# Softmax factors through DRAM, a reordered end of the last layer, and a second weight set asked for sooner, in a two-layer hybrid attention encoder

## The chip, the cores and the metric

The kernel runs on one NeuronCore of a Trainium2 chip, as one program. The metric is device microseconds (us) of one execution; lower is better. A core has five engines that run at once, each through its own instructions in order: TensorE (PE in the profile; its weight loads are PEld) multiplies matrices, VectorE (DVE) and ScalarE (ACT) work element by element and read TensorE's results out of PSUM, GpSimd (POOL) works on SBUF alone, and SyncE (SP) issues most transfers. ACT and POOL issue transfers too, and those of POOL can add to what they write. Instructions of different engines wait for each other by semaphores. PSUM has eight banks of 512 fp32 columns by 128 partitions.

## The reference, cut to what matters

For 512 tokens of 1024 channels, two layers do this (all fp32):

```
proj = x @ w_in                      # queries, keys, values of mixers A and B, two gates
oa = banded_attention(qa, ka, va)    # exp(s - m) @ v / denominator; 8 heads
ob = sum over 3 dilated groups g of weight_g * (exp(s_g - m_g) @ v_g / denominator_g)
h  = (sigmoid(gate_a) * (oa @ w_branch_a) + sigmoid(gate_b) * (ob @ w_branch_b)) @ w_out
x  = layer_norm(alpha * x + h) * ln1_g + ln1_b
ple = sigmoid(x @ w_ple_gate + b) * (p @ w_ple)
x  = layer_norm(alpha * x + relu(x @ w_up)**2 @ w_down + ple) * ln2_g + ln2_b
```

What the change touches: the factors of each token and head (1 / denominator for mixer A; for mixer B the group's softmax weight over its denominators) that multiply the attention sums, the last layer norm with the writing of the output, and the hand-over of `p @ w_ple` to the second layer.

## The kernel before, in words

**Products.** Every fp32 operand is cut into a high part that TensorE takes in its faster fp32 mode and a rest (`split`, L236); a product is three matmuls (high by high, rest by high, high by rest; `mm3` L287). Weights come from DRAM in sets of 128x1024, fetched by SP (`fetch` L252) into three buffers `wst`, and split by `prep` (L261) into three buffers `whi`, `wlo`, two sets ahead of their use (`LOOK`). The sets listed in `LATER` are split by ACT and an adding transfer that POOL issues (`split_later`, L240). Most of these sets belong to the attention block.

**Start.** Eight transfers bring x by 128 channels each into `xs` (four buffers), and each is split; the first weight set is asked for after the first of them (L349 to L355), the others as the first products need them. Only where the code says `manual_schedule` is the order of an engine that of the program; elsewhere Tile's scheduler puts each engine's instructions in the order in which its own simulation finds them ready.

**Attention block** (L358 to L889). Projections ("fill") and the steps of attention units are woven into one order for TensorE, written out by hand: a forecast `fc` (L173) keeps a guessed time and guessed busy stretches of the other engines, and a unit's next step is issued when its condition holds in that guess, delayed further by the table `LEAVE`. `unit_a` (L511, four per layer) and `unit_b` (L594, six per layer) do scores, softmax, transposes of the probabilities and the products with v. Their sums lie as heads by tokens (64 channels of two heads on the partitions, tokens in the columns), while the denominators lie as tokens by heads. `widened` (L493) has ACT copy a unit's 8 factors of each token out to 128x512, `token_scaled` (L498) has TensorE transpose them by four 128x128 transposes into a PSUM bank `R`, and DVE multiplies the sums `f` by it. `unit_a` does this once at its end and splits the product into `OA`; `mix_b` (L704, two per layer) does it for each of its three groups and adds the groups up into `OB`. The products with `OA` (`ya`, in the filler) come late in the block and those with `OB` (`yb`) after it.

**Between the layers.** At the end of layer 0, while the last rows are normed, `embedding` (L1096) computes `p @ w_ple` for layer 1 into `ple` tiles that stay in SBUF through the attention of layer 1; rows go to DRAM (`kept`); the first set of the next layer is split with POOL's adding transfer and its product is begun (`start_by_halves`, L322).

**Down products.** `Down` (L974) multiplies by seven products (a scheme of Strassen's kind) for each quarter q of the hidden channels. `product(q, n)` (L1051) runs two row blocks s of 12 matmuls of 512 columns each; `gather` (L1078) then adds each result to y. After the last quarter's product 3, layer 1 ends with products 4, 5 and 6 in this order (L1301 to L1350), both s of each. Rows are four blocks y[0] to y[3] of 128 tokens: product 4 completes y[0] and y[1], products 5 and 6 complete y[2] and y[3]. `Tokens` (L898) has the moments and statistics of the layer norm: DVE's moments by halves, its aggregate, a reciprocal, ACT's square root, one step of refinement; then centring, scaling, adding the last bias, and writing `out`.

## Time and profile before

| | us |
|---|---|
| median of 3 runs (1530.86 to 1531.6) | 1531.06 |
| the profiled execution's own time | 1530.95 |
| its span, first to last instruction | 1529.2 |
| TensorE busy | 1506.9 (99%) |
| VectorE busy | 1030.7 (67%) |
| ScalarE busy | 768.2 (50%) |
| GpSimd busy | 250.9 (16%) |

The profiled execution takes 1.75 us more than its span, for what lies around the first and last instruction. A matmul's row lasts from its start to its modelled end and overlaps the next one's, so what a matmul costs TensorE is read from start to start. A row with "x4" stands for four instructions in a run; its length goes from the first's start to the last's end.

### The profile page before, as it was taken

How to read it: one execution, taken by the hardware profiler on the slowest of the kernel's cores; microseconds unless marked ns; L12 is line 12 of the kernel's file. 1: busy time of each engine (PE TensorE's matmuls, PEld its weight loads, DVE VectorE, ACT ScalarE, POOL GpSimd, SP SyncE). 2: the span in 40 equal slices, each digit the busy share in tenths (PEclk: the TensorE clock that was granted, in tenths of full speed). 3: DMA queues.
4: the chain of work that ended last, by engine and by line, in shares of the span. 5: the costliest groups of instructions: out<-in, count | busy, mean ns of one | idle time of the engine just before them, and what ended most of it. 6: DMA issues, size and time to landing. Idle time of an engine off the chain costs nothing.

```text
span 1529.2 us, 19607 instructions
## 1 busy us (share of the span) xinstructions
PE 1506.9 (99%) x7374; PEld 1249.8 (82%) x7374; DVE 1030.7 (67%) x1761; ACT 768.2 (50%) x1254; POOL 250.9 (16%) x221
## 2 busy tenths in 40 slices
PE   9999999999999999999999999999999999999996
PEld 7888888888888888888888888888888888888885
DVE  5865564458568777686868655544585876767868
ACT  5887674344344443444558776643442444444342
POOL 1221220110011120202022112211100201111022
PEclk9999999999999999999999999999999999999998
DMA  7644655345612414151455456565455233231403
GB/s 243 144 109 117 147 138 191 99 138 152 206 56 86 135 53 155 42 159 62 105 169 138 113 123 150 126 188 156 150 151 181 69 110 111 85 123 56 150 0 97
DMA packets 54592, 190.52 MB, mean 125 GB/s; under 512 B 6625, under 2 KB 7009, under 8 KB 54497
## 3 DMA queue, kind: packets, MB, share of 16 engines
q1 hardware_dynamic: 43200, 151.74, 29.8%
q0 software_dynamic: 10576, 37.23, 13.0%
q8 instruction: 58, 0.95, 0.2%
q10 hardware_dynamic: 720, 0.30, 0.1%
q14 instruction: 38, 0.30, 0.1%
HBM read 155.16 MB, written 4.19 MB: 104 GB/s over the span
## 4 chain that ended last, share of the span: by engine, by line
PE 87%; DVE 6%; ACT 2%; DMA 2%; issue 2%; POOL 0%; SPq 0%; POOLq 0%; ACTq 0%; DVEq 0%
PE dn L1065 17%; PE ps_up L291 8%; PE ps_up L289 8%; PE ps_up L290 8%; PE wo L297 2%; PE pg L297 2%; PE pg L295 2%; PE pg L296 2%; PE wo L296 2%; PE wo L295 2%; PE pta L451 1%; PE sb L473 1%; PE sa L478 1%; PE ya L289 1%; PE ya L291 1%
## 5 line engine op out<-in xcount | busy, mean ns | idle before, releaser
L237 ACT CAST whi<-wst 128x1024 fp32r<-128x1024 f32 (+2 forms) x120 | 121.1, 1010 | 261.6 <-PE ps_up L290 115.4
L238 DVE TENSOR_TENSOR wlo<-wst,whi 128x1024 fp32r<-128x1024 f32 (+2 forms) x120 | 146.1, 1222 | 142.3 <-ACT whi L237 131.9
L289 PE MATMUL ps_up<-xhi,whi 128*128 128x512 f32 x512 | 199.2, 389 | 0.0
L290 PE MATMUL ps_up<-xlo,whi 128*128 128x512 f32 x512 | 199.2, 389 | 0.0
L291 PE MATMUL ps_up<-xhi,wlo 128*128 128x512 f32 x512 | 199.2, 389 | 0.0
L1038 POOL TENSOR_TENSOR hr<-r 128x512 f32<-128x512 f32 x64 | 102.2, 1597 | 550.2 <-ACT r L1030 529.7
L290 PEld LDWEIGHTS ps_up<-xlo,whi 128*128 128x128 f32 x512 | 96.1, 188 | 20.0
L291 PEld LDWEIGHTS ps_up<-xhi,wlo 128*128 128x128 f32 x512 | 96.1, 188 | 19.9
L289 PEld LDWEIGHTS ps_up<-xhi,whi 128*128 128x128 f32 x512 | 96.1, 188 | 19.9
L237 ACT CAST whi<-raw 128x1024 fp32r<-128x1024 f32 x56 | 58.0, 1052 | 97.0 <-PE ps_up L290 64.1
L237 ACT CAST dhi<-raw 128x1024 fp32r<-128x1024 f32 x56 | 58.7, 1052 | 82.2 <-PE dn L1065 59.5
L1084 DVE TENSOR_TENSOR y<-y,dn 128x512 f32<-128x512 f32 x96 | 65.2, 682 | 38.5 <-PE dn L1065 38.5
L244 POOL DMA_DIRECT2D wlo<-wst x54 | 47.8, 885 | 253.6 <-ACT wlo L243 150.9
L1018 DVE TENSOR_TENSOR raw<-raw,raw 128x1024 f32<-128x1024 f32 x64 | 86.4, 1350 | 0.2
L238 DVE TENSOR_TENSOR wlo<-raw,whi 128x1024 fp32r<-128x1024 f32 x56 | 68.2, 1220 | 14.1 <-ACT whi L237 14.1
L238 DVE TENSOR_TENSOR dlo<-raw,dhi 128x1024 fp32r<-128x1024 f32 x56 | 69.2, 1239 | 5.4 <-ACT dhi L237 5.4
L242 ACT CAST whi<-wst 128x1024 fp32r<-128x1024 f32 x54 | 56.5, 1046 | 30.3 <-PE ps_start L290 6.9
L243 ACT ACTIVATE wlo<-whi 128x1024 fp32r<-128x1024 f32 x54 | 57.3, 1061 | 0.8
L1065 PE MATMUL dn<-whi,smh 128*128 128x512 f32 x128 | 50.2, 394 | 0.7 <-DVE y L1084 0.7
L1065 PE MATMUL dn<-wlo,smh 128*128 128x512 f32 x128 | 50.5, 395 | 0.1
L1065 PE MATMUL dn<-whi,sml 128*128 128x512 f32 x128 | 49.9, 390 | 0.0
L1065 PE MATMUL dn<-dhi,smh 128*128 128x512 f32 x128 | 49.9, 390 | 0.0
(860 smaller groups left out, 4049.2 us busy)
## 6 DMA issues: line engine op xcount, KB each, us to landing
wst<-wst SPq DMA_DIRECT2D x187, 512.0 KB, 3.5
raw<-wst SPq DMA_DIRECT2D x64, 512.0 KB, 4.3
wlo<-wst POOLq DMA_DIRECT2D x54, 512.0 KB, 4.6
y<-rows POOLq DMA_DIRECT2D x14, 512.0 KB, 7.7
row<-rows SPq DMA_DIRECT2D x7, 512.0 KB, 8.4
wst<-wst SPq DMA_DIRECT2D x9, 256.0 KB, 2.7
xs<-xT SPq DMA_DIRECT2D x8, 256.0 KB, 6.2
y<-xN SPq DMA_DIRECT2D x4, 512.0 KB, 6.6
```

The lines of the kernel that those rows point to most:

```text
L237: nc.scalar.copy(hi, src)
L238: nc.vector.tensor_tensor(lo, src, hi.bitcast(F32), ALU.subtract)
L289: nc.tensor.matmul(ps, w[0][:, s], x[0], start=start, stop=False, skip_group_check=part)
L290: nc.tensor.matmul(ps, w[0][:, s], x[1], start=False, stop=False, skip_group_check=part)
L291: nc.tensor.matmul(ps, w[1][:, s], x[0], start=False, stop=stop, skip_group_check=part)
L295: nc.tensor.matmul(ps, x[0], w[0][:, c], start=start, stop=False)
L296: nc.tensor.matmul(ps, x[0], w[1][:, c], start=False, stop=False)
L297: nc.tensor.matmul(ps, x[1], w[0][:, c], start=False, stop=stop)
L1018: nc.vector.tensor_tensor(to, to, other, ALU.add)
L1038: nc.gpsimd.tensor_tensor(h.rearrange("p s t -> p (s t)"), r, r, ALU.mult)
L1065: nc.tensor.matmul(ps[s], a[:, k, tok], w[b][:, cols], start=first and not (k or m), stop=k == 3 and m == 2, skip_group_check=True)
L1084: return nc.vector.tensor_tensor(to, to, ps, ALU.subtract if n in (2, 4, 5) else ALU.add)
```

## The change

In the attention block a unit's factors are transposed as they are, 8 (mixer A) or 24 (mixer B) columns at once, by one transpose (`in_rows`); ACT copies the rows to SBUF and issues a transfer of them to DRAM; SP issues two transfers for each 128x512 tile `R`, which read a row of factors and repeat it over 64 partitions (`in_columns`). The multiplication by `R` and what follows it are put off by `LATENCY` = 7 us of the forecast (`scaled_a`, `mixed_b`); `f` has two buffers and `R` three. The first products with `OA` wait in the written order for the put-off steps. `LEAVE` is another table, of 34 entries where there were 26.

At the start `xs` has eight buffers, and the second weight set is asked for after the second piece of x.

At the end of layer 0 the `ple` tiles are written to DRAM (four of 256 KB) and read back in layer 1 after its attention.

The end of layer 1 goes by row block: product 4 for s = 0, product 5 for s = 0, product 4 for s = 1, product 6 for s = 0, then products 5 and 6 for s = 1 in halves of 256 columns. `out[0]` and `out[1]` are filled beforehand with the last bias, and y[0] and y[1] leave by POOL's adding transfers. y[2] is transposed by TensorE; ACT applies the last scale and bias by channel, and it is written transposed, which the host turns back. For y[3] DVE does the rest. To give product 5 its weights in time, the order of two splits beside product 3 of the last quarter is exchanged.

```diff
+LATENCY = 7
...
 LEAVE = {
-    ("a", 0, 1): 0.6, ("a", 0, 14): 0.6, ("a", 1, 4): 0.3, ("a", 1, 16): 4.5, ("a", 2, 18): 1.0,
...
+    ("a", 0, 1): 2.2, ("a", 0, 11): 2.2, ("a", 0, 14): 1.5, ("a", 0, 16): 1.5, ("a", 1, 4): 1.0,
...
-        with tc.tile_pool(name="xp", bufs=4) as xp:
+        with tc.tile_pool(name="xp", bufs=8) as xp:
             for k in range(KT):
                 xs = xp.tile([P, S], F32, tag="xs", name=f"xs{k}")
                 nc.sync.dma_start(xs, xT[:, k, :])
                 if k == 0:
                     ahead(0)
                 split(X[k][0], X[k][1], xs)
+                if k == 1:
+                    ahead(1)
...
-            def widened(c, name, after):
-                wide = av.tile([P, 4, 2, 64], F32, tag="wide", name="wide" + name, bufs=1)
-                nc.scalar.copy(wide, c.rearrange("p r (j u) -> p j r u", u=1).to_broadcast([P, 4, 2, 64]))
-                return wide, fc.on("act", 0.52, after) + HOP
...
-            def token_scaled(f, wide, name, after):
-                R = bank("pt", "rs" + name)
-                for j in range(4):
-                    nc.tensor.transpose(R[:, j * P:(j + 1) * P], wide[:, j].rearrange("p r d -> p (r d)"), ident)
...
+            def in_rows(c, n, name, after):
+                tp = bank("pt", "rt" + name)
+                nc.tensor.transpose(tp[:n, :P], c, ident)
+                r = av.tile([24, P], F32, tag="rt", name="rt" + name, bufs=1)
+                nc.scalar.copy(r[:n], tp[:n, :P])
+                t = fc.on("act", 0.3, fc.pe(0.11) + HOP) + HOP
+                fc.take("pt", t)
+                line = dp.tile([24, P], F32, tag="line", name="line" + name, bufs=2)
+                nc.scalar.dma_start(line[:n], r[:n])
+                return line, max(t, after) + LATENCY
+            def in_columns(line, name):
+                R = av.tile([P, S], F32, tag="wide", name="R" + name, bufs=3)
+                for r in range(2):
+                    nc.sync.dma_start(R[r * 64:r * 64 + 64, :],
+                                      line[r * 4:r * 4 + 4].rearrange("j p -> (j p)").partition_broadcast(64))
+                return R
+            def scaled_a(i, f, R, t):
+                yield lambda: fc.t >= t
                 nc.vector.tensor_tensor(f, f, R, ALU.mult)
+                split(OA[i][0], OA[i][1], f)
+                forecast_split(S, fc.on("dve", 0.7, fc.t))
+                del held["oa", i]
+            def mixed_b(sp, fs, Rs, t):
+                yield lambda: fc.t >= t
+                for (f, _, _), R in zip(fs, Rs):
+                    nc.vector.tensor_tensor(f, f, R, ALU.mult)
+                f = fs[0][0]
+                nc.gpsimd.tensor_tensor(f, f, fs[1][0], ALU.add)
+                nc.vector.tensor_tensor(f, f, fs[2][0], ALU.add)
+                split(OB[sp][0], OB[sp][1], f)
...
-                wide, t_wide = widened(den, nm_, ex[1, 3] + 0.6)
+                t_den = ex[1, 3] + 0.6
+                held["oa", i] = True
                 yield lambda: "va" in held
                 v, t_v = held["va"]
-                f = av.tile([P, S], F32, tag="f", name="f" + nm_, bufs=1)
+                f = av.tile([P, S], F32, tag="f", name="f" + nm_, bufs=2)
                 groups = [(r, kbs) for r in range(2) for kbs in ((0, 3), (1,), (2,))]
...
-                yield lambda: fc.open("pt") and fc.t >= t_wide
-                t_f = token_scaled(f, wide, nm_, t_f)
-                split(OA[i][0], OA[i][1], f)
-                forecast_split(S, t_f)
+                yield lambda: fc.open("pt") and fc.t >= t_den
+                line, t = in_rows(den.rearrange("p r j -> p (r j)"), 8, nm_, t_f)
+                side.append([scaled_a(i, f, in_columns(line, nm_), t), None, ("oa", i), 0])
...
-                for g in range(3):
-                    f, t_f, _ = fs[g]
-                    wide, t = widened(e[:, g].rearrange("p (s b) -> p s b", s=2), f"{nm_}_{g}", t)
-                    yield lambda: fc.t >= t and fc.open("pt")
-                    token_scaled(f, wide, f"{nm_}_{g}", t_f)
-                    t = fc.t
-                f = fs[0][0]
-                nc.gpsimd.tensor_tensor(f, f, fs[1][0], ALU.add)
-                nc.vector.tensor_tensor(f, f, fs[2][0], ALU.add)
-                split(OB[sp][0], OB[sp][1], f)
+                yield lambda: fc.t >= t and fc.open("pt")
+                line, t = in_rows(e.rearrange("p g b -> p (g b)"), 24, nm_, t)
+                Rs = [in_columns(line[8 * g:8 * g + 8], f"{nm_}_{g}") for g in range(3)]
+                side.append([mixed_b(sp, fs, Rs, t), None, ("ob", sp), 0])
...
-                        yield lambda: not any(k[0] == "a" for k in (*waiting, *live))
+                        yield lambda: not any(k[0] in ("a", "oa") for k in (*waiting, *live, *held))
...
+            def in_two(self, *args, **kw):
+                steps = self.steps(*args, **kw)
+                next(steps)
+                return lambda: next(steps, None)
+            def steps(self, a, n=2, root=False, centre=True):
                 sm = self.pool.tile([P, 6, 2], F32, tag="nsm", name=f"nsm{self.name}_{a}", bufs=2)
...
-                for i in range(n):
+                for i in range(n if centre else 0):
                     nc.scalar.activation(self.y[a + i], self.y[a + i], AF.Identity, bias=m[:, i:i + 1])
+                if centre is None:
+                    self.weighed(a, 0)
+                yield
...
+                if centre is None:
+                    self.weighed(a, 1)
+                elif not centre:
+                    nc.vector.scalar_tensor_tensor(h, self.mv[:, a:a + n, 0], -1.0, r, ALU.mult, ALU.mult)
+                    for i in range(n):
+                        for y in (self.y[a + i][:, :512], self.y[a + i][:, 512:]):
+                            nc.scalar.activation(y, y, AF.Identity, bias=h[:, i:i + 1], scale=self.rs[a + i])
...
+            def weighed(self, a, h):
+                c = slice(h * 512, (h + 1) * 512)
+                nc.vector.scalar_tensor_tensor(self.y[a][:, c], self.y[a][:, c], self.mv[:, a, 0:1], self.g[:, c],
+                                               ALU.subtract, ALU.mult)
...
+            def half(self, q, n, s, c0=0, c1=512):
...
+                if c0:
+                    self.bank[tag, s] = self.bank.get((tag, s)) or bank("mm", f"dn{self.l}_{q}_{n}_{s}_{c0}")
+                ps = (self.bank[tag, s] if c0 else self.bank[tag][s])[:, c0:c1]
+                tok = slice(s * P, (s + 1) * P)
+                for c in range(2):
+                    w = self.sets[n, c]
+                    for i in range(2):
...
+        kept_ple = [dp.tile([P, S], F32, tag=f"keptple{a}", name=f"keptple{a}", bufs=1) for a in range(4)]
...
+            for a in range(4 if l else 0):
+                ple[0, a] = np1.tile([P, S], F32, tag="ple0", name=f"ple{l}_0_{a}", bufs=4)
+                nc.sync.dma_start(ple[0, a], kept_ple[a])
...
-                                if s:
+                                if s != (last and q == FQ - 1 and n == 3):
                                     dn.cut(q, n + 2, 0)
...
+                    with tc.issue_after(dn.ready.ins):
+                        for a in range(2):
+                            nc.sync.dma_start(out[a], rows[l, 4].partition_broadcast(P))
+                    tn.g = g2
+                    def taken(n, s, *cols):
+                        dn.gather(q, n, s, dn.half(q, n, s, *cols), *cols)
+                    def weighed(a):
+                        for c in (slice(0, 512), slice(512, D)):
+                            nc.gpsimd.tensor_tensor(y[a][:, c], y[a][:, c], g2[:, c], ALU.mult)
+                        nc.gpsimd.dma_start(out[a], y[a], accum_op=ALU.add)
+                    z = qp.tile([P, KT, P], F32, name="z", tag="raw110", bufs=1)
+                    def turned_out(a, h, tag):
+                        tp = bank(tag, f"out{a}_{h}")
+                        ks = range(4 * h, 4 * h + 4)
+                        for i, k in enumerate(ks):
+                            nc.tensor.transpose(tp[:, i * P:(i + 1) * P], y[a][:, k * P:(k + 1) * P], ident)
+                        for i, k in enumerate(ks):
+                            nc.scalar.activation(z[:, k], tp[:, i * P:(i + 1) * P], AF.Identity, bias=b2[:, k:k + 1],
+                                                 scale=gc[:, k:k + 1])
+                        to = out[a].rearrange("(p k) (j t) -> p (k j) t", k=1, j=KT)
+                        nc.sync.dma_start(to[:, ks.start:ks.stop], z[:, ks.start:ks.stop])
+                    def roots(a):
+                        return tn.in_two(a, 1, root=True, centre=False)
+                    taken(4, 0)
+                    tn.moments(0, 1)
+                    rest = roots(0)
+                    taken(5, 0)
+                    tn.moments(2, 1)
+                    rest()
+                    weighed(0)
+                    taken(4, 1)
+                    tn.moments(1, 1)
+                    rest = roots(1)
+                    taken(6, 0)
+                    tn.moments(2, 0)
+                    rest()
+                    weighed(1)
+                    for n, h in ((5, 2), (6, 0)):
+                        for i in range(2):
+                            taken(n, 1, i * 256, i * 256 + 256)
+                            tn.moments(3, h + i, 4)
+                            if h + i == 2:
+                                rest = roots(2)
+                            if not h + i:
+                                rest()
+                    rest = tn.in_two(3, 1, root=True, centre=None)
+                    rest()
+                    for h, tag in enumerate(("pt", "o")):
+                        turned_out(2, h, tag)
+                    for h, issue in enumerate((nc.sync, nc.scalar)):
+                        c = slice(h * 512, (h + 1) * 512)
+                        nc.vector.scalar_tensor_tensor(y[3][:, c], y[3][:, c], tn.rs[3], b2r[:, c], ALU.mult, ALU.add)
+                        issue.dma_start(out[3][:, c], y[3][:, c])
...
-                    embedding(l + 1, 0, PL, p0, range(2, 4))
+                    embedding(l + 1, 0, PL, p1, range(2, 4))
+                    for a in range(4):
+                        nc.sync.dma_start(kept_ple[a], ple[0, a])
...
                     begun = start_by_halves(l + 1, second)
+                    p1_close()
...
-    return np.asarray(r.results[0]["out"]).reshape(1, S, D)
+    o = np.array(r.results[0]["out"])
+    o[2] = o[2].reshape(P, KT, P).transpose(2, 1, 0).reshape(P, D)
+    return o.reshape(1, S, D)
```

## Rows read from the trace of the kernel before

**Rows 1.** The profile's page: its busy times (share of the span, instructions), and the chain that ended last, by engine.

```profile
PE 1506.9 (99%) x7374; PEld 1249.8 (82%) x7374; DVE 1030.7 (67%) x1761; ACT 768.2 (50%) x1254; POOL 250.9 (16%) x221
...
PE 87%; DVE 6%; ACT 2%; DMA 2%; issue 2%; POOL 0%; SPq 0%; POOLq 0%; ACTq 0%; DVEq 0%
```

**Rows 2.** Two stretches inside the attention blocks of layer 0 and layer 1: length, TensorE's busy time and instructions, granted clock, busy share of the 16 DMA engines, GB/s.

```profile
30.00:240.00 210.00, 208.49 (x1241) 1.00 0.53 129
790.00:1000.00 210.00, 208.31 (x1229) 1.00 0.54 131
```

**Rows 3.** All waits of TensorE in the span: total us, times, the longest.

```profile
PE ps_start L291 <- DMA wlo<-wst: 1.5, 1, 1.5
...
PE rs L501 <- ACT wide L495: 0.8, 2, 0.4
PE ps_start L289 <- ACT whi L237: 0.6, 1, 0.6
```

**Rows 4.** The end of layer 1 in order of time: TensorE's last matmul, VectorE, ACT, POOL, and SP's last transfer.

```profile
1515.41 0.39 PE L1065 MATMUL dn<-dhi,axl 128*128 128x512 f32 x1
...
1504.21 0.68 DVE L1084 TENSOR_TENSOR y<-y,dn 128x512 f32<-128x512 f32 x1
...
1505.53 0.67 DVE L1084 TENSOR_TENSOR y<-y,dn 128x512 f32<-128x512 f32 x1
...
1514.96 0.21 DVE L915 BATCH_NORM_AGGREGATE nmvn<-nstn 128x2 f32<-128x12 f32 x1
...
1516.27 0.16 DVE L926 SCALAR_TENSOR_TENSOR nsmn<-nsmn 128x1 f32<-128x1 f32 x1
...
1519.99 0.75 DVE L943 SCALAR_TENSOR_TENSOR y<-y,nsmn,row 128x512 f32<-128x512 f32 x1
...
1523.76 0.69 DVE L1349 TENSOR_TENSOR y<-y,row 128x512 f32<-128x512 f32 x1
...
1515.76 1.13 ACT L922 ACTIVATE y<-y,nsmn 128x1024 f32<-128x1024 f32 x1
...
1511.22 3.53 POOL L1329 TENSOR_TENSOR y<-y,row 128x512 f32<-128x512 f32 x2 [31.72 <-ACT y L1327]
...
1524.52 0.97 SPq L1350 DMA_DIRECT2D out<-y  x1
```

**Rows 5.** TensorE in order of time around one of `token_scaled`'s transposes: start, length, line, operation.

```profile
250.04 0.60 PE L501 MATMUL rs<-ident,wide 128*128 128x128 f32 x4
250.39 0.48 PE L289 MATMUL ya<-oah,whi 128*128 128x512 f32 x1
250.71 0.39 PE L290 MATMUL ya<-oal,whi 128*128 128x512 f32 x1
250.94 0.40 PE L291 MATMUL ya<-oah,wlo 128*128 128x512 f32 x1
```

**Rows 6.** TensorE's groups by line and shape: those of `token_scaled` (count, busy us, mean ns, idle before).

```profile
L501 PE MATMUL rs<-ident,wide 128*128 128x128 f32 x48 | 7.3, 274 | 0.8 <-ACT wide L495 0.8
L501 PE MATMUL rsa<-ident,widea 128*128 128x128 f32 x32 | 4.8, 272 | 0.0
```

**Rows 7.** Layer 0, one tile each: the transposed factors of mixer A, the first products with `OA`, the transposed factors of mixer B, the first products with `OB` (ns min/median/max, start of the first and the last).

```profile
L501 PE MATMUL rsa<-ident,widea x16: 270/272/273, 72.1 to 135.5; 128*128 128x128 f32 x16
...
L289 PE MATMUL ya<-oah,whi x32: 389/389/504, 237.6 to 272.7; 128*128 128x512 f32 x32
...
L501 PE MATMUL rs<-ident,wide x24: 270/272/328, 197.7 to 252.2; 128*128 128x128 f32 x24
...
L289 PE MATMUL yb<-obh,whi x16: 389/389/389, 284.3 to 327.1; 128*128 128x512 f32 x16
```

**Rows 8.** SP's own waits before it issues a transfer, from 30 to 260 us: total us, times, the longest.

```profile
SPq L258 <- DMA wlo<-wst: 208.6, 26, 13.6
```

**Rows 9.** Transfers from 30 to 260 us by line: count, KB each, median us from issue to landing. Each of these two copies 64 partitions, 128 KB, within SBUF.

```profile
qh1ka<-qh1ka POOLq DMA_DIRECT2D x1, 128.0 KB, 5.8
...
ql1ka<-ql1ka POOLq DMA_DIRECT2D x1, 128.0 KB, 2.5
```

**Rows 10.** The start in order of time, TensorE and then ACT.

```profile
12.10 0.39 PE L291 MATMUL ps_start<-xhi,wlo 128*128 128x512 f32 x1
13.09 0.50 PE L289 MATMUL ps_start<-xhi,whi 128*128 128x512 f32 x1 [0.60 <-ACT whi L237]
...
11.99 1.05 ACT L237 CAST whi<-wst 128x1024 fp32r<-128x1024 f32 x1 [0.66 <-DMA wst<-wst]
```

**Rows 11.** The passage from layer 0 to layer 1 in order of time, ACT's copies of `ple` and then TensorE's first products of layer 1, of 256 columns.

```profile
759.99 0.60 ACT L1104 ACTIVATE ple<-ple 128x512 f32<-128x512 f32 x1 [3.46 <-PE ple L297]
761.36 0.60 ACT L1104 ACTIVATE ple<-ple 128x512 f32<-128x512 f32 x1 [0.77 <-PE ple L297]
...
767.79 0.28 PE L289 MATMUL ps_start<-xhi,whi 128*128 128x256 f32 x1
767.91 0.27 PE L290 MATMUL ps_start<-xlo,whi 128*128 128x256 f32 x1
```

**Rows 12.** Transfers from 754 to 768 us: the hardware queue (packets, MB, share of 16 engines), and POOL's adding transfer of the first weight set (KB, us to landing).

```profile
q1 hardware_dynamic: 576, 2.56, 60.1%
...
wlo<-wst POOLq DMA_DIRECT2D x1, 512.0 KB, 10.6
```

**Rows 13.** Transfers from 1490 to 1531 us: POOL's adding transfers (KB each, median us to landing).

```profile
y<-rows POOLq DMA_DIRECT2D x2, 512.0 KB, 6.2
```

More of the change, by code (lines that the diff above doesn't have):

```diff
@@ L1352, in build, with fifth @@
+                    def fifth(s):
+                        tn.moments(2 + s, 1)
+                        if not s:
+                            tn.statistics(0)
+                            return
+                        ahead(at[0] + 1)
+                        tn.scaled(0, g2)
+                        tn.scaled(1, g2)
+                    dn.product(q, 5, fifth)
                     PL = [(ph[:, k], pl[:, k]) for k in range(2)]
```

111 lines of the change are left out of this document (34 added, 77 removed), and 11 rows, old and new, of the table LEAVE.

## The prediction, made before the changed kernel ran

> **What bounds the kernel now.** I read the page first: TensorE is busy 1506.9 of 1529.2 us, and 87% of the chain that ended last is TensorE's [rows 1]. So a matmul removed is time removed, unless something else comes late. Next the stretches where the change lies: inside both attention blocks TensorE is busy over 208 of 210 us at the full granted clock (1.00, the 2.4 GHz level), with the DMA engines about half busy [rows 2]. Its named waits are few: 1.5 us for POOL's adding transfer at the passage between the layers, 0.8 us for ACT's `wide` copies, 0.6 us for the second weight set at the start [rows 3]. What is left is the end: TensorE's last matmul ends at 1515.8 [rows 4], the span at 1529.2, so 13.4 us hold no matmul. The sum below has therefore four places: fewer transposes, the start, the passage, the end.
>
> **Transposes removed.** The durations in a group's row overlap, so I take starts. Four transposes start at 250.04 and the next matmul at 250.39: 0.35 us. That next matmul holds its successor off for 0.32 us, where the following distance is 0.23: 0.09 more. One group of four costs TensorE 0.44 us [rows 5]. The groups have 48 and 32 transposes, 20 groups [rows 6]: 8.8 us go. Added are 12 single transposes (4 mixer A units and 2 mixes, twice). No row shows a single one of this kind: it costs at least a quarter of 0.35 (0.09, 1.1 us in all) and at most a whole group (0.44, 5.3 us); I take 0.09 plus the 0.09 after it, 0.18, since the second part is paid for each change of work: 2.2 us. Net 6.6 us, bounds 3.5 to 7.7. The 0.8 us of waits for `wide` [rows 3] go as well, since the new transpose reads the factors themselves: 7.4 us. Nothing covers TensorE here, so all of it should show.
>
> The Trainium skill (TensorE: Matmul & The Clock Gate, Part 4: PE-mode transpose) gives about 275 ns to a transpose within a kernel. By that figure 80 less 12 transposes would be worth 18.7 us. The trace has the same 272 to 274 ns as a row's length, but the starts stand 0.09 apart, so the measurement decides for 6.6.
>
> **What the way through DRAM adds.** ACT loses 20 copies and gains 12 small ones with an issue each; it is half idle [rows 1], so nothing. The results are needed late: mixer A's last factors are used at 135.5 us and `ya` begins at 237.6; mixer B's last at 252.2 and `yb` at 284.3, 32 us [rows 7]. So the longer way does not reach the products. It can reach TensorE by the queues. SP waited 208.6 of 230 us for POOL's transfers to free `wst`, 8.0 us on average, 13.6 at most [rows 8]: an `R` transfer that stands behind such a wait is late, and a weight fetch behind an `R` transfer waits for ACT and the row. In DVE's order the multiplication waits for `R`; behind it stand the masks and splits that TensorE needs within a few microseconds. The program puts it off by 7 us. Two transfers of the nearest kind take 2.5 to 5.8 us each [rows 9], 5.0 to 11.6 in a row. At the middle, 8.3, DVE is held 1.3 us per unit, 12 times, and TensorE has filler products meanwhile. I take nothing, with bounds 0 and 12 times 1.3, 16 us.
>
> The Trainium skill (DMA: Bandwidth & Descriptors, Anatomy of one DMA) states a fixed 2.0 us, most of it the receipt of the last write, plus bytes over 436 GB/s. By that, an estimate, the pair takes 4.3 us and nothing is ever held; no row of before shows this pair, and the sum goes by the row bounds.
>
> The new `LEAVE` table changes no instruction, only when steps are issued. It can win at most the few waits left in attention and lose about as much: 0, bounds -2 and +3.
>
> **Start.** The second set is split by ACT from 11.99 on, when it lands; TensorE's last matmul of the first set starts at 12.10, and the next at 13.09 instead of 12.33 [rows 10]. Asked for before six pieces of x it should land over a microsecond sooner: 0.76 us go, I take 0.7. What is late next is x's third and fourth piece, pushed back by 512 KB; bounds 0.8 gained and 1 lost.
>
> **Passage.** Four `ple` writes of 256 KB join SP's queue. ACT has the first two ready at 760.6 and 762.0 [rows 11], while POOL's adding transfer of the first weight set, which TensorE already waits 1.5 us for, takes 10.6 us from issue to landing beside 2.56 MB of hardware transfers (60.1% of 14 us, 8.4 us) [rows 12]. Half a MB more at that rate is 1.6 us; it may come too late to matter. I take +1.2, bounds 0 and 3.2 (all four). The reading back, in layer 1, comes long before its use and costs nothing; if it were late, the first gated rows would wait for it.
>
> **End.** 24 matmuls of 512 columns become 48 of 256. From start to start that is 0.12 us for 256 [rows 11] against 0.23: +0.2, so TensorE ends at 1516.0. DVE turns to these products at 1504.21 in both kernels, behind the last weight splits. One gather with its moments takes 1.32 us (1504.21 to 1505.53); a chain from the aggregate to the refined root 1.47 (1514.96 to 1516.43) [rows 4]. Before the last half DVE has 4 x 1.32 + 3 x 0.8 (half the columns, an estimate) + 3 x 1.47 = 12.1 us, to 1516.3, about when TensorE ends. Then gather and moments, 0.8, to 1517.1; the chain and four passes of 0.75 over half a row, 4.5 in all: DVE ends at 1521.6 instead of 1524.45. From there to the span's end were 4.73 us; I keep them: 1526.3, gain 2.9. y[2] takes another way: ACT's 1.13 for the row, transposes, eight copies; I put it about 1 us sooner. y[1] leaves by POOL: DVE has its root by 1504.21 + 4 x 1.32 + 2 x 1.47 = 1512.4, ACT is done at 1513.6, two products of 1.77 end at 1517.1, and 6.2 to landing [rows 13] make 1523.3. Bounds of the gain: 1.5 (that landing takes the 10.6 of rows 12, to 1527.7) and 5 (a landing as short as the 2.5 of rows 9).
>
> **Sum.** 1529.2 - 7.4 - 0.7 + 1.2 - 2.9 = 1519.4 of span; with the 1.75 around it 1521.15 for this execution, which lies 0.1 below the median: 1521.3.
>
> **The rivals.** (a) As summed; with the bounds partly against each other, 1516 to 1526: 0.72. (b) DVE is held at the multiplications by 8.3 - 7 = 1.3 us, and half of it reaches TensorE, 12 x 0.65 = 7.8: 1529.1, or 1526.5 at a third. For it: DVE's order is fixed before the landing is known. Against it: 7 us of room, and products of x that need nothing from DVE. 0.12. (c) The end hardly moves: POOL's adding transfers or y[2]'s transposed write land last, at 1527.7: 1522.7. For it: the 10.6 us landing; against it: at the end only four writes of 256 KB stand beside. 0.10. (d) Slower, by SP's order: an `R` transfer behind a fetch that waits 8.0 us starts that much later, DVE waits 8.0 + 5.0 - 7 = 6.0 us per unit, and TensorE loses a third of it, 12 x 2.0 = 24: 1545. It outweighs the gain from 0.8 us per unit on, and is slower by over 0.2% from 1.1. For it: the 208.6 us of waits. Against it: where Tile sets the order, a transfer is placed when its simulation has it ready, and the fetches run ahead of their need. 0.06.
>
> **How the numbers follow.** 0.2%, 3 us, is about what a measurement of this kernel can tell from no change. Faster is (a), (c) and about half of (b): 0.88. Within 0.2% the rest of (b): 0.06. Slower: (d), 0.06. The range leaves out the top of (b), (d) and the lowest corner of (a): 1515.5 to 1526.5.
>
> **What would show it.** Right: no 128x512 `wide` copies, new transposes at about 0.2 us from start to start; TensorE busy 208 of 210 us in attention still; the wait for `wlo` at the passage at 2 to 3 us; no wait for `whi` at 13; DVE's last operation some 5.6 us after TensorE's last product, and the span's end some 10 us after it instead of 13.4. Wrong: idle time of TensorE behind DVE's multiplications by `R`, fetches of SP that come late after them, or a span's end set by POOL's transfers.

## The result and the profile after

The changed kernel takes 1537.59 us (median of 6 runs); the kernel before took 1530.74 beside it. The ratio is 1.005 (95% interval 1.004 to 1.0061): some 7 us slower, where 1521.3 was forecast. The profiled execution of that comparison, 1541.98, is the longest of its six, 4.4 above their median, and its granted clock reads 0.943 over the span, where the other five have 0.995 to 0.997. So I had the same kernel profiled a second time (run e0_again, 1535.97, median 1536.68, clock 0.997). All rows of "after" come from this second profile.

> The changed kernel once more, nothing edited, as a second profile. Its six timed runs lay at 1536.0 to 1542.0 and the profiled one was the longest, 1542.0. If the losses read from that profile belong to the kernel, this one shows them too: DVE held at the multiplications by R about 16 times, some 46 us in all, and about 7 us lost at the first gate of branch b in layer 1, at a time near 1537.5. If the 4.5 us above the median were made by that execution alone, one of these is clearly smaller here.

The losses are the kernel's own: both profiles show them (in branch b of layer 1, told of below, 6.9 us in the first and 5.3 in the second). The lower reading of the clock hardly shows in the products: the 435 us to the last `up` took 435.2 in the first and 434.9 in the second. The ledger cuts the span at TensorE's landmarks; each figure is a difference of starts in the view by tile (us): the first start, for `up` the last one, and for the last product its modelled end. Its columns are the kernel before, the changed kernel, and four experiments told of below.

| stretch | before | after | e1 | e2 | e4 | e9 |
|---|---|---|---|---|---|---|
| start to the transposes of `vt` | 29.6 | 27.3 | 27.7 | 28.2 | 28.0 | 29.0 |
| attention of layer 0, to `yb` | 254.7 | 258.4 | 258.8 | 251.8 | 251.7 | 252.0 |
| to the last `up` | 434.6 | 434.9 | 435.1 | 435.2 | 435.4 | 434.9 |
| passage, to `vt` of layer 1 | 73.0 | 71.2 | 71.1 | 71.2 | 71.1 | 71.0 |
| attention of layer 1, to `yb` | 254.9 | 257.8 | 255.0 | 250.8 | 250.8 | 250.8 |
| branch b of layer 1, to `wo` | 43.5 | 48.8 | 43.7 | 53.3 | 48.3 | 43.6 |
| to the last `up` | 385.9 | 386.2 | 386.9 | 386.0 | 387.0 | 387.1 |
| to the end of the last product | 39.6 | 40.0 | 40.0 | 40.0 | 39.9 | 40.0 |
| to the span's end | 13.4 | 9.6 | 9.7 | 9.4 | 9.5 | 9.5 |
| span | 1529.2 | 1534.2 | 1528.0 | 1525.9 | 1521.7 | 1517.9 |

Start, passage and end gained 2.3, 1.8 and 3.8 us. Three stretches lost: attention 3.7 and 2.9, branch b of layer 1 5.3.

Attention first, in windows of the same length as in [rows 2] (us, busy time and instructions by engine, granted clock, DMA share, GB/s):

```profile
30.00:240.00 210.00, 202.01 (x1193) 167.57 (x1193) 132.21 (x371) 147.03 (x326) 44.69 (x52) 1.00 0.59 140
790.00:1000.00 210.00, 203.44 (x1180) 169.29 (x1179) 135.24 (x377) 148.52 (x327) 47.25 (x53) 0.99 0.58 137
```

TensorE is busy for 202 and 203 us, where it was over 208. The granted clock is 1.00 in the first, the 2.4 GHz level. The 0.99 of the second is a mean and hides a stretch at the lower level, 1.2 GHz: after a wait of 2.5 us that ends at 864.9, the clock is 0.50 until about 868. In two of those microseconds TensorE has 7 instructions, where it had 16 from 860 to 862:

```profile
866.00:868.00 2.00, 2.00 (x7) 1.52 (x7) 1.90 (x7) 1.21 (x5) 0.00 (x0) 0.50 0.10 41
```

Half of that stretch, about 1.7 us, is an estimate of what it costs, out of the 2.9 that layer 1 lost. A wait of 2.8 us in layer 0, up to 101.6, was not followed by one: the rows from 100 to 108 read 1.00. TensorE's longest waits, against [rows 3] (total, times, longest):

```profile
PE sa L482 <- DVE mxa L470: 5.3, 2, 2.8
PE ps_('g', 1, 2)_9484 L291 <- ACT gate L913: 3.5, 1, 3.5
PE ob L487 <- DVE ptlb L240: 2.5, 2, 1.2
PE ptb L455 <- ACT pb L466: 2.0, 2, 1.0
PE ob L486 <- DVE ogb L492: 1.6, 2, 1.0
PE ob L716 <- DVE ogb L492: 1.5, 2, 0.7
```

Four of the six end with DVE. Before, the first was 0.9 and the fourth 0.4, and the other four did not exist. The waits for `wide` and for `whi` of [rows 3] are gone, as forecast. The wait for `wlo` is gone too, where a longer one, 2 to 3 us, was forecast. The next view is DVE's own waits, those for a transfer:

```profile
DVE fa L518 <- DMA Ra<-linea: 28.6, 8, 5.9
...
DVE ogb L526 <- DMA R<-line: 20.0, 9, 5.9
```

DVE stands 17 times in front of a multiplication by `R`, 48.6 us in all, 2.9 each. One of them in order of time (start, length, engine, line, operation; in brackets the idle time before it and what ended it):

```profile
91.02 0.25 ACT L502 COPY rta<-rta 8x128 f32<-8x128 f32 x1
91.30 0.28 ACTq L506 DMA_DIRECT2D linea<-rta  x1
94.16 1.35 SPq L512 DMA_DIRECT2D Ra<-linea  x2
95.32 0.55 DVE L470 CUSTOM_DVE_ANT_0 pa<-sa,ct 128x384 f32<-128x384 f32 x1
95.79 0.08 DVE L470 DVE_READ_ACCUMULATOR2_ANT mxa<- 128x1 f32 x1
100.41 0.69 DVE L518 TENSOR_TENSOR fa<-fa,Ra 128x512 f32<-128x512 f32 x1 [4.53 <-DMA Ra<-linea]
101.02 0.55 DVE L470 CUSTOM_DVE_ANT_0 pa<-sa,ct 128x384 f32<-128x384 f32 x1
...
101.63 0.44 PE L482 MATMUL sa<-qh1ka,ql_qa 128*128 128x384 f32 x1 [2.76 <-DVE mxa L470]
```

From ACT's issue to the multiplication are 9.1 us: 2.9 until SP may issue, 1.35 for two issues, 4.9 until `Ra` is there. DVE reaches the multiplication at 95.87, 4.6 us after ACT's issue. Over the 12 units the way to the first multiplication takes 6.3 to 9.8 us, 7.9 in the middle, and DVE is there 3.6 to 5.3 us after the issue. It stands between the two masks of one pair: the second, at 101.02, is what TensorE's next scores wait for.

The other loss. Branch b of layer 1 took 43.5 us before. First SP's reading of `y` before, then SP and ACT after:

```profile
1016.78 3.79 SPq L1128 DMA_DIRECT2D y<-kept  x4
```

```profile
1014.91 5.39 SPq L512 DMA_DIRECT2D R<-line  x6
1020.68 3.76 SPq L260 DMA_DIRECT2D wst<-wst  x2
1024.54 1.80 SPq L1182 DMA_DIRECT2D y<-kept  x4
1029.46 0.33 SPq L260 DMA_DIRECT2D wst<-wst  x1
1029.84 0.42 SPq L1213 DMA_DIRECT2D pf<-pT  x1
1030.32 0.92 SPq L1015 DMA_DIRECT2D row<-rows  x2
1031.28 2.78 SPq L1219 DMA_DIRECT2D ple<-keptple  x4
...
1053.01 1.04 ACT L239 CAST whi<-wst 128x1024 fp32r<-128x1024 f32 x1 [7.97 <-DMA wst<-wst]
...
1055.24 0.68 ACT L913 ACTIVATE gate<-ps_('g', 1, 1)_9419,vhalf 128x512 f32<-128x512 f32 x1
```

The four new transfers of `ple` stand with those of `y`, `pf` and the rows in front of the next weight fetches. ACT waits 8 us for a weight set at 1053; the gate's activation is queued behind it, and TensorE waits 3.5 us for that gate (the second row of its waits). The rest of the 5.3 is again the clock, 0.50 from 1055.9 to 1059.3, about 1.7 us by half of that time (the same columns as above; the last but one is the DMA share):

```profile
1046.00:1048.00 2.00, 2.00 (x11) 1.65 (x10) 0.00 (x0) 0.00 (x0) 0.00 (x0) 1.00 1.07 243
...
1056.00:1058.00 2.00, 2.00 (x5) 1.61 (x6) 2.00 (x4) 0.43 (x1) 0.72 (x1) 0.50 0.82 227
```

The DMA share is about 1 from 1026 to 1052 (1.04 on average): all 16 engines are full while the weight set is on its way.

The end, against [rows 4]:

```profile
1524.82 0.89 POOL L1375 DMA_DIRECT2D out<-y  x1 [0.41 <-POOL y L1374]
1524.30 0.28 PE L1122 MATMUL dn<-dhi,axl 128*128 128x256 f32 x1
1528.17 1.41 DVE L1421 SCALAR_TENSOR_TENSOR y<-y,nsmn,row 128x512 f32<-128x512 f32 x2
1529.60 0.33 SPq L1388 DMA_DIRECT2D out<-z  x1
1529.62 0.37 ACTq L1422 DMA_DIRECT2D out<-y  x1
```

DVE ends 5.0 us after TensorE's last product (1529.58 to 1524.58), the span 9.6.

### The profile page after: what moved, and what is told of

Read it like the earlier page. It is cut to its first block, busy times and chain, and to the rows that moved or that the text cites. A ratio compares the mean times of both kernels' runs of the same rounds, so it can differ in the third digit from the quotient of the medians.

```text
span 1540.2 us, 19635 instructions
## 1 busy us (share of the span) xinstructions
PE 1508.7 (98%) x7338; PEld 1247.7 (81%) x7338; DVE 1028.4 (67%) x1768; ACT 760.9 (49%) x1256; POOL 251.9 (16%) x220
## 4 chain that ended last, share of the span: by engine, by line
PE 83%; DVE 6%; DMA 5%; ACT 3%; issue 1%; POOL 0%; SPq 0%; DVEq 0%; POOLq 0%; ACTq 0%
PE dn L1122 17%; PE ps_up L291 8%; PE ps_up L293 8%; PE ps_up L292 8%; PE pg L299 2%; PE wo L299 2%; PE wo L297 2%; PE wo L298 2%; PE pg L297 2%; PE pg L298 2%; DMA Ra<-linea 1%; PE sb L477 1%; PE ps_start L291 1%; PE ps_start L292 1%; PE ps_start L293 1%
## 5 line engine op out<-in xcount | busy, mean ns | idle before, releaser
L239 ACT CAST whi<-raw 128x1024 fp32r<-128x1024 f32 x56 | 58.0, 1053 | 97.0 <-PE ps_up L292 57.7
L1138 DVE TENSOR_TENSOR y<-y,dn 128x512 f32<-128x512 f32 (+1 forms) x98 | 65.3, 670 | 38.3 <-PE dn L1122 38.3
L1122 PE MATMUL dn<-whi,smh 128*128 128x512 f32 (+1 forms) x130 | 50.5, 391 | 0.7 <-DVE y L1138 0.7
L1122 PE MATMUL dn<-wlo,smh 128*128 128x512 f32 (+1 forms) x130 | 50.9, 392 | 0.1
L1122 PE MATMUL dn<-whi,sml 128*128 128x512 f32 (+1 forms) x130 | 50.3, 387 | 0.0
L299 PE MATMUL pg<-bhi,xlo 128*128 128x512 f32 x128 | 49.9, 390 | 0.3 <-DVE xlo L1010 0.3
```

The source lines that it names most:

```text
L239: nc.scalar.copy(hi, src)
L299: nc.tensor.matmul(ps, x[1], w[0][:, c], start=False, stop=stop)
L1122: nc.tensor.matmul(ps, a[:, k, tok], w[b][:, cols], start=first and not (k or m), stop=k == 3 and m == 2, skip_group_check=True)
L1138: return nc.vector.tensor_tensor(to, to, ps, ALU.subtract if n in (2, 4, 5) else ALU.add)
```

## The experiments

My theory after these rows: the way through DRAM makes the loss in attention, because DVE is held at the multiplications; and the reading back of `ple` makes the loss in branch b. Rivals: the new table of pauses; the transfers themselves as a load; SP's queue late as a whole.

**e1: the old way of the factors.** `widened` and `token_scaled` with the table of before; start, passage, parking of `ple` and end as changed.

```
...
-line, t = in_rows(den.rearrange("p r j -> p (r j)"), 8, nm_, t_f)
-side.append([scaled_a(i, f, in_columns(line, nm_), t), None, ("oa", i), 0])
...
+t_f = token_scaled(f, wide, nm_, t_f)
+split(OA[i][0], OA[i][1], f)
...
```

> The changed kernel with the token factors made as before (wide copies, groups of four transposes, multiplied at once) and the table of before; start, passage, parking of ple and end stay as changed. Theory 1 (the way through DRAM loses the time inside attention, and the read-back of ple some 7 us at the first gate of layer 1's branch b by itself): attention as before, start -1.0, passage -1.7, end -4.0, read-back +6.9, so 1530.7 + 0.2 = 1530.9. Rival (the read-back is only late because the R transfers and the late attention pushed SP's queue back): 1524.0. Second rival (the loss inside attention has nothing to do with the factors): above 1535.

Measured: 1529.81, ratio to before 0.9998 (0.9989 to 1.0006), 6.9 under the changed kernel. The sum came close to the theory's 1530.9, but not by its items. Branch b takes 43.7 us although `ple` is read back: that loss needs the new factors as well. Layer 1's attention is back at 255.0. Layer 0's is not: 258.8, with a wait of TensorE that the kernel before had at 0.2 us:

```profile
PE sa L481 <- DMA ql0ka<-ql0ka: 3.1, 2, 2.4
```

So start, passage and end together (1.9, 1.9 and 3.7 us here) are worth nothing measurable with the old factors and the old table: layer 0's attention gives 4.1 us back, the other stretches 2.2. The wait grew because the transfer of `ql0ka`, issued 1.6 us earlier than before (35.1 against 36.7), landed 4.7 us after its issue, not 2.7. All of TensorE's idle time in that block is 2.4 us longer than before, and a stretch at 0.50 (41.3 to 44.7) follows the wait, some 1.7 us by half of it: together the 4.1. Why the transfer took longer is not shown.

**e2: the multiplications later on DVE.** TensorE's order is the same, matmul for matmul; DVE's changes, ACT's follows it, and a few weight fetches and one reading of `ple` change places on SP. `newest['dve']` is the mask or split that the program gave DVE last.

```
...
+yield lambda: fc.t >= t + 6
+with tc.issue_after(newest['dve'].ins):
     nc.vector.tensor_tensor(f, f, R, ALU.mult)
...
```

> The changed kernel with one thing moved: the multiplications by R are put behind the mask or split that the plan has reached 6 us later, so that DVE does that work first. TensorE's order is the same, matmul for matmul. Theory 1 (DVE held at the multiplications, 46 us in 16 waits, makes the loss inside attention): the waits shrink below 10 us and the attention blocks get back most of what they lost, 9.1 us against before and up to 16.5 with the transposes' gain, so 1521 to 1529. Rival (the new table of pauses, or the transfers themselves, make the loss): the waits shrink and the time stays at 1536 to 1538.

Measured: 1527.13, ratio 0.9976 (0.9967 to 0.9985): 9.5 us faster than the changed kernel. No wait of DVE for `R` is left, and TensorE is busy in the two windows for

```profile
30.00:240.00 210.00, 207.20 (x1224) 173.18 (x1224) 136.52 (x384) 151.13 (x331) 46.30 (x53) 1.00 0.59 140
790.00:1000.00 210.00, 207.71 (x1229) 173.91 (x1228) 136.15 (x386) 150.51 (x330) 44.91 (x52) 1.00 0.59 139
```

The DMA share is still 0.59: the transfers as a load cost nothing that shows. The two attention blocks take 6.6 and 7.0 us less than in the changed kernel, and 2.9 and 4.1 less than before: 7.0 us of gain, where 7.4 was forecast. A single new transpose, in order of time:

```profile
90.38 0.27 PE L502 MATMUL rta<-ident,dena 128*8 128x128 f32 x1
90.41 0.48 PE L293 MATMUL ps_('g', 0, 2)_908<-xhi,whi 128*128 128x512 f32 x1
90.72 0.39 PE L294 MATMUL ps_('g', 0, 2)_908<-xlo,whi 128*128 128x512 f32 x1
```

0.03 to the next start, and that matmul 0.31 instead of 0.23: 0.11 us. But branch b got worse, 53.3 us: TensorE comes to it 12.4 us earlier (1037.2 against 1049.6), but `y` is read only 6.3 us earlier (1018.3 against 1024.5).

```profile
PE ps_('g', 1, 2)_9484 L293 <- ACT gate L918: 6.7, 1, 6.7
```

The clock is 0.50 after it until 1052.8, 6 us beyond the end of the wait: 6.7 and about 3.0 are the 9.8 that the stretch lost.

How the multiplication came to stand too early can be read from the built program, without a run: putting it 3, 5, 8 or 40 us later in the written plan, without the pin, leaves the order on TensorE, DVE, ACT and SP as it was. The written plan orders TensorE alone; DVE's place comes from Tile's own estimate. The 7 us of `LATENCY` never reach DVE. No run has a larger `LATENCY`: with 12 the written plan comes to no complete order.

**e3: `ple` read back later.**

```
-            for a in range(4 if l else 0):
...
-                nc.sync.dma_start(ple[0, a], kept_ple[a])
...
                 for a in range(4):
                     projected(a, 0, pss[a])
+                if l:
+                    with tc.issue_after(newest[0].ins):
+                        for a in range(4):
...
+                            nc.sync.dma_start(ple[0, a], kept_ple[a])
```

`newest[0]` (`at_sp[0]` from e4 on) is the weight fetch issued last in the program's text at that point.

> The changed kernel with the reading back of ple moved: its four transfers stand on SP behind the weight fetches of the first half of w_out, not ahead of the fetches of branch b. Theory 1 (those four transfers and the pf and row loads, in front of the fetch of the second gate's weights, make the 8.3 us wait of ACT at 1057): the stage from yb to w_out in layer 1 gets back 3.8 to 6.9 us, so 1530.7 to 1533.8. Rival (the fetch is late by itself, because wst buffers come free late and y is read back there too): no change, 1536 to 1538.

Measured: 1534.11, ratio 1.0024 (1.0015 to 1.0033), 2.6 under the changed kernel. Branch b takes 44.5 us (1051.8 to 1096.3) instead of 48.8, so the stretch gave back 4.3, in the expected range, and no lower clock is left in it. The time is 0.3 above the range that was expected for it; the start of that profile was 1.4 later.

**e4: both moves,** the edits of e2 and e3 together.

> The changed kernel with both moves together: the multiplications by R pinned 6 us later on DVE, and the reading back of ple behind the fetches for w_out. Theory (two separate losses, each removed): the pinned kernel's 1527.1 less what its stage from yb to w_out in layer 1 lost, 53.3 us against 43.5 before, so 1517.3 to 1518.3, some 3 to 4 below what the prediction had for the change. Rival (the weight fetches there are late through the reading of y and pf, not of ple): only the 2.6 of the move alone, 1524.5.

Measured: 1523.34, ratio 0.995 (0.9937 to 0.9964). The theory's number is missed by 5 us; the rival's 1524.5 lies within the interval (1521.1 to 1525.2). Branch b takes 48.3 us, 5.0 under e2's and still 4.8 over the 43.5: TensorE waits 2.9 us for the gate, and the clock at 0.50 from 1043.5 to 1046.9 makes about 1.7. In e6 and e7, which have the same edits there, it takes 50.2 and 50.0, so what the move of `ple` gives back there is 3.1 to 5.0. ACT still waits for a weight set, and SP shows what stands in front of it:

```profile
1018.01 2.03 SPq L1189 DMA_DIRECT2D y<-kept  x4
1020.10 0.45 SPq L1220 DMA_DIRECT2D pf<-pT  x1
1020.59 0.96 SPq L1022 DMA_DIRECT2D row<-rows  x2
...
1041.08 1.04 ACT L241 CAST whi<-wst 128x1024 fp32r<-128x1024 f32 x1 [7.92 <-DMA wst<-wst]
```

`y` is read at 1018.0, 19.0 us ahead of `yb` (1037.0). Before, it was 30.0 (1016.8 to 1046.8). The same loads now collide with the second gate's weights. SP has issued `y`, `pf` and the rows within 3.5 us, but the DMA engines are full from 1020 to 1042 (share 1.04), and a weight fetch issued at 1033.9 lands 10.9 us later, where 4.0 is the middle. Before, the same burst (1.01 from 1022 to 1044) was over when `yb` began. Besides these loads it holds four transfers of POOL that add a row to `y`, 512 KB each.

**e9: `y`, `pf` and the rows later too,** and with `y` the four adding transfers of POOL (`add_row`).

```
-                nc.sync.dma_start(y[a], kept[a] if l else xN[a])
-                if l:
-                    add_row(y[a], l - 1, 4)
...
+                if l and u in (1, 2):
+                    with tc.issue_after(at_sp[0].ins):
+                        for a in (2 * u - 2, 2 * u - 1):
+                            nc.sync.dma_start(y[a], kept[a])
+                    for a in (2 * u - 2, 2 * u - 1):
+                        add_row(y[a], l - 1, 4)
...
+            with tc.issue_after(at_sp[0].ins):
                 nc.sync.dma_start(pf, pT[l])
                 bg, g1 = row(np1, l, 0, "bg"), row(np1, l, 1, "g1")
...
```

> Both moves, and in layer 1 the reading of y, of pf and of the two rows also put behind weight fetches of branch b's gates (the adding of the row to y goes with it). In the run with both moves the stage from yb to w_out still took 48.3 us against 43.5 before. Theory (these 4 MB start where mixer B's last multiplication frees the memory, which now is only 19 us ahead of yb and not 30, and stand in front of the second gate's weights): the stage comes back to 43.5 to 44.5, so 1523.3 - 4.3 = about 1519 (1518 to 1520). Rival (the fetch is late through its buffer, not through these transfers): no difference, 1523; and if y comes too late for the first w_out sums, slower than 1523.

Measured: 1518.0, ratio 0.9915 (0.9902 to 0.9929), 12.9 us faster than before. TensorE is busy through all of branch b at a clock of 1.00, with the DMA engines at 0.80 (first row) instead of 0.31 before (second row):

```profile
1037.70:1081.30 43.60, 43.60 (x194) 36.10 (x194) 24.22 (x24) 18.14 (x25) 12.46 (x10) 1.00 0.80 229
```

```profile
1046.80:1090.30 43.50, 43.50 (x193) 36.04 (x192) 23.00 (x23) 17.12 (x23) 8.97 (x6) 1.00 0.31 103
```

So the loss there was a matter of when these bytes move, not of how many they are: from 1016 to 1042 the DMA share is now 0.26. Which of the loads did it, `y` with POOL's adding transfers, `pf` or the rows, is not taken apart. (With the sizes of the profile `y`, `pf` and the rows are 3.5 MB, not the 4 of the expectation.)

**e5, e10, e11: the table.** e4 with the table of before; e4 with an empty one; the kernel before with an empty one. No run has the new table with the old factors: the written plan comes to no complete order there.

```
e10:
-LEAVE = {
-    ("a", 0, 1): 2.2, ("a", 0, 11): 2.2, ("a", 0, 14): 1.5, ("a", 0, 16): 1.5, ("a", 1, 4): 1.0,
...
+LEAVE = {}
```

> Both moves (pinned multiplications, ple read back later), and the table of pauses of before in place of the new one. The prediction's term for the table was 0, bounds -2 and +3: so within 3 us of the run with both moves alone. Rival (the order of units needs the new table now that the factors go through DRAM, so that part of the gain belongs to it): more than 3 us slower than that run.

> Both moves, with an empty table of pauses. With the table of before this kernel took 8.3 us more. Theory (a table is fitted to one set of unit lengths, and the old one is just wrong for the new units): the empty table lies near the old one or better, 4 to 9 us slower than the run with both moves. Rival (the new order needs its pauses, and any other table loses the gain): well over 9 us slower.

> The kernel before with an empty table of pauses, so that the worth of its own table is seen. If the old table was worth about as much to the old units as the new one is to the new units, this is 5 to 9 us slower than before, and the table's change cancels out of the comparison of the two kernels. If it was worth little (under 3 us), some 5 us of what the changed kernel would gain without its late transfers are the table's and not those of the removed transposes.

Measured: 1531.63, 1533.64 and 1544.26: 8.3 and 10.3 over e4, and 13.4 over before. Each table is worth 10 to 13 us to its own units. The old one in the new order is worth 2.0 (1533.64 to 1531.63). e5 is the rival's case, far over the 3; e10's 10.3 lies just past the 9 that was set between its theories, and e11's 13.4 is above its 5 to 9. Each expectation was too low by the same mistake: I took the tables for small. In the profiles part of the 8.3 and 10.3 is the clock: e5 and e10 have a stretch at 0.50 in layer 0 that e4 has not (from 41.6 and 40.6 us on), e10 another one in layer 1 (from 962.2). Since a table of similar worth stands on both sides, the comparison of the two kernels holds little of it; that the two worths cancel exactly is not shown.

**e6: the start of before, with both moves.**

```
-        with tc.tile_pool(name="xp", bufs=8) as xp:
+        with tc.tile_pool(name="xp", bufs=4) as xp:
...
-                if k == 1:
-                    ahead(1)
```

> Both moves, and the start of before (four buffers for the pieces of x, second weight set asked for behind them). By the prediction's term this is 0.7 us slower than the run with both moves; by the landmarks of the five profiles with the changed start (first transposes of vt at 27.3 to 28.7 us against 29.6) it is 0.9 to 2.3 slower. Rival (the earlier set only moves the wait on to the pieces of x or to the first rotated q): no difference.

Measured: 1524.92 against 1523.34, 1.6 slower, but the intervals overlap (0.9949 to 0.9973 and 0.9937 to 0.9964). The first transposes of `vt` come at 28.9 against 28.0. Of the 2.5 us between the two profiled spans 1.9 lie in branch b of layer 1, which the edit leaves alone (TensorE's wait there is 4.1 us instead of 2.9, and the clock is back at 1049.4 instead of 1046.9), so the start's own part is the 0.9. In all profiles the transposes come at 28.9 to 29.6 with the start of before (four) and at 27.3 to 29.0 with the changed one (ten). It agrees with a gain of about 1 us and doesn't size it better.

**e7 and e8: the passage.** Both ask where its 1.8 us come from: e7 puts the writes of `ple` behind the last write of `y`; e8 takes the kernel before and puts the constants' load there.

```
e7:
-                    for a in range(4):
-                        nc.sync.dma_start(kept_ple[a], ple[0, a])
...
+                        with tc.issue_after(k23.ins):
+                            for a in range(4):
+                                nc.sync.dma_start(kept_ple[a], ple[0, a])
e8:
+                if l:
+                    with tc.issue_after(at_kept[0].ins):
+                        nc.sync.dma_start(ct, cst[:, :off])
...
```

`k23` and `at_kept[0]` are the last write of `y` to DRAM.

> Both moves, and the four writes of ple to DRAM at the passage put behind the last write of y, so that they no longer stand ahead of the loading of the constants (960 KB). Theory (the passage gained 1.8 us because the writes of ple push that load away from POOL's adding transfer, which TensorE waited 1.5 us for in the kernel before): the load moves back beside that transfer and the wait returns, +1.5 to +1.8. Rival (the gain comes from other work in that stage): 0, or a little faster since four transfers leave the busy stretch.

> The kernel before with one transfer moved: the loading of the constants in layer 1 (960 KB) stands behind the last two writes of y, not between the first two beside POOL's adding transfer. Theory (the passage gained 1.7 to 1.8 us in the changed kernel because that load came later there, away from the adding transfer): the 1.5 us wait for wlo goes, so 1.5 to 1.8 faster than before. Rival (the passage gained by the place of the ple writes or of the products): no difference.

e7: 1522.98, no different from e4. It tells nothing of the theory, because the load did not move back; it was issued at 771.6 us, where before it was 757.1 and in e4 763.0. e8: first the load before, then SP's order in e8:

```profile
757.08 0.38 SPq L366 DMA_DIRECT2D ct<-cst  x1
```

```profile
756.80 1.81 SPq L1360 DMA_DIRECT2D kept<-y  x2
763.57 1.81 SPq L258 DMA_DIRECT2D wst<-wst  x2
769.48 1.52 SPq L1380 DMA_DIRECT2D kept<-y  x2
771.11 0.40 SPq L368 DMA_DIRECT2D ct<-cst  x1
```

with the load at 771.1 instead of 757.1. POOL's adding transfer of `wlo` lands 6.4 us after its issue instead of 10.6, the wait for it is gone, and the passage takes 71.2 instead of 73.0: the mechanism is shown. The time, 1530.54 (ratio 0.9998, 0.9989 to 1.0007), doesn't show it: the stretch from `wo` to the last `up` took 387.2 there against 385.9, so whether the 1.8 us last to the end of that kernel stays open.

## Why the prediction was wrong

**The failed step: "I take nothing" for the way through DRAM.** The bounds, 0 and 16, held the truth: without the holds attention gains 7.0 us (e2), with them it loses 6.6, so they cost 13.6 (9.5 as idle time of TensorE, about 1.7 as the lower clock after one of its waits, the rest within its busy time). Three readings led to the "nothing". "The program puts it off by 7 us": it puts off TensorE's plan; DVE reached the multiplication 3.6 to 5.3 us after the issue. "At the middle, 8.3": 7.9, close. And "DVE is held 1.3 us per unit, 12 times" became 2.9 us, 17 times. "TensorE has filler products meanwhile" was partly right: of 48.6 us of hold 13.6 reached TensorE, 0.28, not the half of rival (b). Rival (b) was the mechanism, with 48.6 us in place of its 15.6. The Trainium skill (DMA: Bandwidth & Descriptors, Anatomy of one DMA) was cited for a pair in 4.3 us, an estimate by which nothing is held. That section of the Trainium skill is about transfers that GpSimd issues, and here ACT and SP issue them. The trace has 6.3 to 9.8, and there the measurement decides.

**The second: "The reading back, in layer 1, comes long before its use and costs nothing".** It was priced by who waits for `ple`; those rows were never late. What counted is what stands behind it, on SP and in the DMA engines. And it is not `ple` alone: with the old factors the same reading costs 0.2 us (e1, 43.7). The loss of 5.3 comes when the factors' transfers are ahead in SP's queue and `y`, `pf`, the rows and `ple` follow so shortly before branch b. e3 and e4 remove `ple`'s part, 4.3 and 3.1 to 5.0; e9 the rest. About a third of the loss is the clock after TensorE's wait (1.7 of 5.3), a cost that no term of the prediction had. "The longer way does not reach the products" looked 32 us ahead for the results, and missed the loads that used this room.

**Rival (d), SP's order, was half right:** SP waits for the row (26.2 us in 6 waits for `linea`, 30 to 1060 us). But its first issue comes 1.2 to 4.4 us after ACT's in all 12 units, so no `R` stood for 8.0 us behind a fetch, and no fetch delayed by that held TensorE inside attention; with DVE's order changed and TensorE's left as it was, all of the loss there went (e2).

**What was right.** Transposes, with the waits for `wide`: 7.4 forecast, 7.0 measured in e2; the added ones cost 0.11, not 0.18. That the sum is so near is partly luck: over both blocks TensorE's busy time fell by 8.9 us where 6.6 was forecast, and its idle time rose by 1.9 where 0.8 was to go; and e2 has another table and another order on DVE as well. End: 3.8 less from the last product to the span's end, and 0.4 more before it, net 3.4 against 2.9. DVE's last operation ends 5.0 after the product, where 5.6 was named, and the span's end comes 9.6 after it, for "some 10". POOL's adding transfers did not set it (rival (c) falls). y[2], put about 1 us sooner, is not sooner: its last write is issued at 1529.60, y[3]'s at 1529.62. Start: about 1 us (0.9 in e6) for 0.7; the 2.3 of the second profile is partly scatter.

**Passage: the sign was wrong.** +1.2 was taken for four more writes; the stretch got 1.8 shorter in every profile of the changed kernel and its variants. I had looked at the bytes added beside POOL's adding transfer and not at the 960 KB of constants that would leave it (e8).

**Table: "0, bounds -2 and +3".** As a change alone it is neither: the new order needs it by 8.3 us, and the old order needs its own.

Together: e9 has every part of the change and three moves in the queues. Its profiled span, 1517.9, is 1.5 under the 1519.4 of the sum: the passage came out 3.2 and the end 0.6 better, attention 0.6, the start 0.1 and the other stretches 1.6 worse. Its median, 1518.0, is 3.3 under the forecast. So the sum was near for a kernel whose queues are in another order than the one it was made for, and it was near by errors that offset each other.

## What to carry to other kernels

When an operand gets a longer way, price it by the queue of the engine that takes it: find the instruction behind the first use, and who waits for that. A delay that is written into the plan of one engine doesn't order another one; if an order matters, pin it. And a load that comes "long before its use" is still in front of something in its queue: when one stage gets faster, look at what then arrives too late for the next. Look at the granted clock behind each wait of TensorE too: here a few waits of 2.5 to 6.7 us cost about half as much again (1.7 to 3.0 us).

## What the runs showed of the hardware that was not expected

A round through DRAM, 4 KB out and 128 KB twice back, took 9.1 us from the issue on ACT to the first use, 2.9 of it until SP could issue; over the 12 units 6.3 to 9.8. The loads of `y`, `pf` and the rows that cost 4.8 us in front of a weight fetch (e4) cost nothing behind it, in a stretch where the DMA engines then were 0.80 busy (e9). After some of TensorE's waits, of 2.5 to 6.7 us, the granted clock was 0.50 for a while, with 5 to 7 instructions in 2 us instead of 10 to 16; another wait of 2.8 us was not followed by this. And a load of 960 KB moved 14 us away from an adding transfer of POOL took that transfer's wait of 1.5 us out of the chain (e8).
